# Storing mixer outputs already split in two words, and moving a block's last sums, conditioning loads and weight remainders, in a streaming encoder layer

## The chip, the cores and the metric

The kernel runs on one core of a Trainium2 chip. The metric is the device time of one execution in microseconds. Several executions are timed and the median is given; one further execution is recorded by the hardware profiler.

## The reference

One layer of a hybrid encoder processes a prompt of 2048 tokens and 8 short samples of 16 tokens. A projection feeds two head groups (a gated delta rule and a band attention), their outputs go side by side through `w_out`, and a two-layer FFN follows. The conditioning vector `c` gives shifts, scales and gates through `w_mod`.

```python
sh1, sc1, g1, sh2, sc2, g2 = split(silu(c) @ w_mod + b_mod, 6)
h = rmsnorm(x, norm1_g) * (1 + sc1) + sh1
proj = h @ w_in                                  # 1024 -> 3592 columns
o_a, conv_state, s = mixer_a(proj, ...)          # 4 heads x 128: conv, delta rule, gated norm
o_b = band_attention(proj, ...)                  # 8 heads x 64: own chunk and 8 chunks before
x = x + g1 * (concatenate([o_a, o_b]) @ w_out)
h = rmsnorm(x, norm2_g) * (1 + sc2) + sh2
x = x + g2 * (square(relu(h @ w_up)) @ w_down)   # 1024 -> 4096 -> 1024
```

All is float32, with outputs for the tokens, the states and the newest keys and values.

## The kernel before

Tokens lie in 17 tiles of 128: 16 of the prompt, and tile 16 (`SMP`), which holds all samples. The large products keep float32 precision with words of the type float32r: a number is split into a high word (a cast, on ScalarE) and a low word (the remainder, by a subtraction), and a product is three matmuls, high by high, high by low and low by high (`mm3`). `hT` holds the transposed input of a product, both words, for the tiles of one block.

Weights come by `weights`: the raw slice of 128 x 1024 is loaded into `raw` (3 buffers), ScalarE casts the high word, and GpSimd subtracts for the low word. The first block that meets a slice may store its low word in DRAM (`s_w_in` and others); later blocks then load that word instead of making it. For `w_in`, block 0 makes and stores the low words, and all later blocks load them.

Phase 1 goes through the projections in six blocks, `[0,1,SMP]`, `[2,3,4]`, `[5,6,7]`, `[8,9,10]`, `[11,12,13]` and `[14,15]`. `proj_a` makes the columns of the delta rule (16 slices of `w_in`), `proj_b` those of the attention (12 slices). For the blocks in `LATE` (4 and 2), `proj_b` comes at the end, after that of the last block. The delta rule of earlier blocks (`gdn_*`) is cut into steps that are put between the products (lanes of generators, called by `tick`); so is the attention of the first two tiles. `gdn_o2` transposes a tile's result and stores it in `s_oa`; the attention stores its results in `s_ob`, head by head. 16 pieces of `w_mod` are used at the start; the other 32 (512 KB each) are loaded one by one by `mod_step`, one in each slot of the q, k and v loop of `proj_a` from block 1 on, until none is left.

Phase 2 has five blocks, `[0,1]`, `[2,3,4]`, and three of four tiles. `out_proj` loads each tile's mixer output from `s_oa` and `s_ob` into a buffer `of` (two buffers), splits it into `hT` on ScalarE and VectorE, multiplies by `w_out`, adds to `x1`, and normalizes. `ffn` then alternates four slices of `w_up` with one group of `w_down` (8 groups, each in two halves of 512 columns), summing the groups in `y` on VectorE. At its end come `y * gate + x1` and the store of `y`. The attention of the next block is spread through the FFN. For a block of four tiles, the products of the last `w_down` group come after the last read of `hT` by `w_up`, so the next block's `hT` can be filled beside them.

The program is written in one order, and a planner in the language (it works from a simulated timeline) puts the instructions of each engine, and the DMAs of each queue, in a fixed order when the kernel is built. Nearly all DMAs are issued by the queue of SyncE, in order; a DMA that waits holds back those behind it.

Of the kernel before, what the change touches and what calls it, by code (L numbers as in the profile page):

```python
# [8 lines left out]
F32 = mybir.dt.float32  # L9
# [42 lines left out]
class Trunk:  # L52
    def __init__(self, ctx, tc, ins, outs):
# [10 lines left out]
        self.s_oa = d("s_oa", (NTILE + 1, P, 4, P))  # L64
        self.s_ob = d("s_ob", (NTILE + 1, P, 4, P))
# [100 lines left out]
    def weights(self, name, k0, c0, a, b):  # L166
# [10 lines left out]
        if key in self.stored:  # L177
            nc.sync.dma_start(w.bitcast(F32)[:, 1, 0:n], kept[self.stored[key]][:, 0:n])
            return v(0), v(1)
        self.tt(w[:, 1, 0:n], r, w[:, 0, 0:n].bitcast(F32), ALU.subtract, eng=nc.gpsimd)  # L180
        if self.keep[name]:
            m = sum(k[0] == name for k in self.stored)
            nc.sync.dma_start(kept[m][:, 0:n], w.bitcast(F32)[:, 1, 0:n])
            self.stored[key] = m
# [283 lines left out]
    def proj_a(self, tiles, hT, nxt=()):  # L468
# [38 lines left out]
        for h in range(AH):  # L507
            kq = self.bp.tile([P, 2, self.nt * P], F32, tag="kq", name="kq", bufs=8)
            blk["kq"].append(kq)
            for sec in (1, 0, 2):  # L510
# [28 lines left out]
                if self.bi:  # L539
                    self.mod_step()  # L540
# [329 lines left out]
    def gdn_o2(self, tl, z):  # L870
# [4 lines left out]
        oT = self.tmp("oT")  # L875
        self.act(oT, pt, AF.Copy, scale=self.gdng)
        nc.sync.dma_start(self.s_oa[tl], g4(oT))
# [135 lines left out]
    def conv_gen(self):  # L1013
        nc = self.nc
        for src, w, dst in ((self.hist, 3, self.o["conv_prompt"][0].rearrange("b w c -> (b w) c")),
                            (self.hists, 24, self.o["conv_sample"][0].rearrange("b w c -> (b w) c"))):
            for g in range(3):
# [3 lines left out]
                t = self.tp.tile([P, 512], F32, tag="oT", name="cst", bufs=1)  # L1021
# [4 lines left out]
    def phase1(self):  # L1026
        nc, tc = self.nc, self.tc
        with ExitStack() as st:
# [27 lines left out]
            for bi, tiles in enumerate(B):  # L1056
# [4 lines left out]
                self.drain_to(bi - 2)  # L1061
                blk = self.proj_a(tiles, self.hT, B[bi + 1] if bi in LATE else ())
# [15 lines left out]
            for b, nb in zip(rest, rest[1:] + [None]):  # L1078
                self.proj_b(B[b], self.hT, B[nb] if nb is not None else ())
# [41 lines left out]
    def attention_first(self, tiles):  # L1121
# [53 lines left out]
        def values(h, PT):  # L1175
# [10 lines left out]
            self.tt(o, o, tm[:, 1], ALU.add)  # L1186
            u = h % 2
            for j in range(n):
                nc.sync.dma_start(self.s_ob[tiles[j]][u * 64:(u + 1) * 64, h // 2], o[:, j])
# [20 lines left out]
    def attention_gen(self, tiles):  # L1210
# [67 lines left out]
        def values(h, t, PT):  # L1278
# [5 lines left out]
            tm = ap.tile([64, 256], F32, tag="otmp", name="otmp", bufs=2)  # L1284
            nc.scalar.copy(tm, pv[64:128, 0:256])
            self.tt(tm, tm, pv[0:64, 0:256], ALU.add)
            o = ap.tile([64, P], F32, tag="of", name="of", bufs=2)
            self.tt(o, tm[:, 0:P], tm[:, P:256], ALU.add)
            u = h % 2
            nc.sync.dma_start(self.s_ob[t][u * 64:(u + 1) * 64, h // 2], o)  # L1290
# [33 lines left out]
    def sample_gen(self):  # L1324
# [91 lines left out]
        nc.sync.dma_start(self.s_ob[SMP], oT)  # L1416
# [10 lines left out]
    def out_proj(self, tiles, gates):  # L1427
# [3 lines left out]
        for j, t in enumerate(tiles):  # L1431
            cs = slice(j * P, (j + 1) * P)
            for q, src in enumerate((self.s_oa, self.s_ob)):
                f = self.hp.tile([P, 4, P], F32, tag="htmp", name="of", bufs=2)
                nc.sync.dma_start(f, src[t])
                ks = slice(4 * q, 4 * q + 4)
                self.split(self.hT[:, ks, 0, cs], self.hT[:, ks, 1, cs], f)
# [57 lines left out]
    def ffn(self, tiles, h2, x1):  # L1495
# [3 lines left out]
        y = [self.fp.tile([P, D], F32, tag="y", name="y", bufs=self.nt) for _ in tiles]  # L1499
        G, NF = NGRP, FF // P  # L1500
        us, made = [], 0
        for fi in range(NF + 1):
# [7 lines left out]
            for half in range(2):  # L1510
                hs = slice(half * 512, (half + 1) * 512)
                ws = self.wslices("w_down", g * G, half * 512, 512, G, 2)
                for j in range(n):
# [6 lines left out]
                    else:  # L1520
                        self.tt(y[j][:, hs], y[j][:, hs], ps, ALU.add)
                    self.tick(3 * G * 512)
            us = us[G:]
        self.drain()
        gates = {t == SMP: None for t in tiles}
        for k in gates:
            gates[k] = self.gate_tile(1, k)
        for j, t in enumerate(tiles):
            self.tt(y[j], y[j], gates[t == SMP], ALU.mult)
            self.tt(y[j], y[j], x1[j], ALU.add)  # L1530
            nc.sync.dma_start(self.y_dst(t), y[j])

    def phase2(self):
        nc, tc = self.nc, self.tc
        with ExitStack() as st:
# [4 lines left out]
            self.hT = self.p2.tile([P, KT, 2, self.nt * P], F32R, name="hT2")  # L1540
            for bi, tiles in enumerate(BLOCKS2):
# [5 lines left out]
                x1 = self.out_proj(tiles, [gates[t == SMP] for t in tiles])  # L1547
                if bi + 1 < len(BLOCKS2):
# [6 lines left out]
    def run(self):  # L1555
        self.nraw, self.nw = 3, 4
        self.deferred, self.lanes, self.pending, self.fill_rate, self.fill_acc = [], ([], [], []), [0, 0, 0], 0.0, 0.0
        self.front, self.solved, self.spent = 0, 0, 0
# [38 lines left out]
```

## Time and profile before

| | |
|---|---|
| median of 3 executions | 3190.09 us (3189.9 to 3201.82) |
| the profiled execution, its own time | 3191.66 us |
| its span, first to last instruction | 3190.0 us |
| TensorE busy | 3060.4 us (96%) |
| VectorE, ScalarE, GpSimd busy | 55%, 46%, 19% |
| mean granted TensorE clock | 0.977 |
| DMA | 747 MB, mean 234 GB/s |

Busy times are sums of instruction durations. Matmuls are pipelined, so TensorE counts as busy a little longer than it works; where the granted clock is below 1, the same work takes longer. A window gives the busy time of each engine in a stretch, and the rest of the stretch is idle time.

### The profile page before, as it was taken

The page shows a single profiled execution, that of the slowest core. Times are in us where ns is not written, and L with a number is a line of the kernel's source. Part 1 is how long each engine was busy: PE and PEld are TensorE (multiplying, and loading weights), DVE is VectorE, ACT ScalarE, POOL GpSimd, SP SyncE. Part 2 cuts the span into 40 slices and gives each one's busy share as a digit, 9 for nine tenths or more (in the row PEclk, how much of TensorE's full clock was granted, in tenths as well). Part 3 has the DMA queues.
Part 4 walks back from the last instruction along what each step waited for, and adds up shares of the span by engine and source line. Part 5 has one row for each costly group of instructions (what it writes and reads, how often), then busy time and mean ns, then how long its engine had stood idle before and what let it go on. Part 6 is the DMA issues. An engine that isn't in the chain of part 4 may idle for free. (4 is left out here: it accounts for less than half of the span.)

```text
span 3190.0 us, 53098 instructions
## 1 busy us (share of the span) xinstructions
PE 3060.4 (96%) x19649; PEld 2717.8 (85%) x19649; DVE 1768.1 (55%) x4358; ACT 1471.8 (46%) x2803; POOL 593.5 (19%) x495
## 2 busy tenths in 40 slices
PE   6999999999999989998999999999999999999998
PEld 5998988899989878887999988888988877888887
DVE  4775677777868664675256652444645433442223
ACT  3554545555556555545345453444355333333222
POOL 3631212120212347642222000000000000000000
PEclk8999999999989989998999999999999999999999
DMA  9799897888888768886777766666766667856664
GB/s 295 238 293 300 260 291 221 264 259 245 275 267 272 217 225 268 252 291 192 247 252 246 254 202 188 201 186 205 236 203 200 214 223 228 272 173 196 192 191 139
DMA packets 629116, 747.44 MB, mean 234 GB/s; under 512 B 59680, under 2 KB 483600, under 8 KB 626808
## 3 DMA queue, kind: packets, MB, share of 16 engines
q1 hardware_dynamic: 623096, 712.58, 70.6%
q0 software_dynamic: 5760, 31.46, 3.1%
q8 instruction: 155, 2.54, 0.3%
q14 instruction: 105, 0.86, 0.1%
HBM read 631.29 MB, written 115.52 MB: 234 GB/s over the span
## 5 line engine op out<-in xcount | busy, mean ns | idle before, releaser
L175 ACT CAST w<-raw 128x1024 fp32r<-128x1024 f32 (+1 forms) x528 | 552.0, 1046 | 381.8 <-PE psd L164 212.5
L1479 PE MATMUL psu<-hT,w 128*128 128x512 f32 (+2 forms) x1328 | 471.6, 357 | 4.8 <-ACT hT L104 4.4
L1480 PE MATMUL psu<-hT,w 128*128 128x512 f32 (+2 forms) x1328 | 470.9, 355 | 0.0
L1481 PE MATMUL psu<-hT,w 128*128 128x512 f32 (+2 forms) x1328 | 469.8, 354 | 0.7 <-DMA w<-s_w_up 0.7
L162 PE MATMUL psd<-w,u 128*128 128x512 f32 x1088 | 430.9, 396 | 0.4 <-DVE y L82 0.4
L164 PE MATMUL psd<-w,u 128*128 128x512 f32 x1088 | 429.7, 396 | 0.2 <-DVE u L82 0.2
L163 PE MATMUL psd<-w,u 128*128 128x512 f32 x1088 | 427.2, 393 | 1.8 <-POOL w L82 1.8
L82 POOL TENSOR_TENSOR w<-raw,w 128x1024 fp32r<-128x1024 f32 (+1 forms) x140 | 338.3, 2428 | 269.5 <-ACT w L175 184.5
L79 DVE SCALAR_TENSOR_TENSOR psu<-psu,r 128x512 f32<-128x512 f32 (+2 forms) x160 | 98.8, 617 | 408.1 <-ACT r L92 407.9
L82 DVE TENSOR_TENSOR y<-y,psd 128x512 f32<-128x512 f32 x238 | 162.5, 685 | 251.9 <-PE psd L164 250.6
L1479 PEld LDWEIGHTS psu<-hT,w 128*128 128x128 f32 x1328 | 251.1, 190 | 36.2 <-ACT hT L104 5.3
L1481 PEld LDWEIGHTS psu<-hT,w 128*128 128x128 f32 x1328 | 251.4, 189 | 32.8 <-DMA w<-s_w_up 1.0
L1480 PEld LDWEIGHTS psu<-hT,w 128*128 128x128 f32 x1328 | 251.7, 190 | 30.5 <-issue 0.8
L164 PEld LDWEIGHTS psd<-w,u 128*128 128x128 f32 x1088 | 204.3, 188 | 47.2 <-issue 0.8
L92 ACT ACTIVATE r<-psu 128x512 f32<-128x512 f32 (+2 forms) x160 | 85.4, 533 | 344.1 <-issue 201.8
L163 PEld LDWEIGHTS psd<-w,u 128*128 128x128 f32 x1088 | 204.8, 188 | 46.1 <-POOL w L82 2.2
L162 PEld LDWEIGHTS psd<-w,u 128*128 128x128 f32 x1088 | 204.5, 188 | 44.6 <-DVE y L82 1.0
L162 PE MATMUL psb<-w,hT 128*128 128x256 f32 x816 | 237.1, 291 | 0.3 <-ACT hT L104 0.3
L164 PE MATMUL psb<-w,hT 128*128 128x256 f32 x816 | 234.3, 288 | 2.4 <-DVE hT L82 1.8
L163 PE MATMUL psb<-w,hT 128*128 128x256 f32 x816 | 234.5, 288 | 0.0
L518 PE MATMUL psq<-hT,w 128*128 128x384 f32 (+1 forms) x576 | 195.9, 340 | 9.0 <-ACT ba L498 8.9
L519 PE MATMUL psq<-hT,w 128*128 128x384 f32 (+1 forms) x576 | 194.2, 337 | 0.0
(316 smaller groups left out, 6492.5 us busy)
## 6 DMA issues: line engine op xcount, KB each, us to landing
raw<-in_w_up_dram SPq DMA_DIRECT2D x160, 512.0 KB
raw<-in_w_down_dram SPq DMA_DIRECT2D x160, 512.0 KB
raw<-in_w_in_dram SPq DMA_DIRECT2D x156, 512.0 KB
w<-s_w_in SPq DMA_DIRECT2D x130, 512.0 KB
w<-s_w_down SPq DMA_DIRECT2D x128, 512.0 KB
w<-s_w_up SPq DMA_DIRECT2D x96, 512.0 KB
raw<-in_w_out_dram SPq DMA_DIRECT2D x40, 512.0 KB
x<-in_x_prompt_dram SPq DMA_DIRECT2D x38, 512.0 KB
```

The lines of the kernel that those rows point to most:

```text
L79: (eng or self.nc.vector).scalar_tensor_tensor(out, in0, scalar, in1, op0, op1)
L82: (eng or self.nc.vector).tensor_tensor(out, in0, in1, op)
L92: self.nc.scalar.activation(out, in_, func, **kw)
L162: mm(out, lh, rh, start=first, stop=False)
L163: mm(out, lh, rl, start=False, stop=False)
L164: mm(out, ll, rh, start=False, stop=last)
L175: nc.scalar.copy(w[:, 0, 0:n], r)
L518: mm(pc, wh, hT[:, k, 0, 0:T], start=(k == 0), stop=False)
L519: mm(pc, wh, hT[:, k, 1, 0:T], start=False, stop=False)
L1479: mm(ps[:, c0:c1], wh, h2[:, k, 0, c0:c1], start=(k == 0), stop=False)
L1480: mm(ps[:, c0:c1], wh, h2[:, k, 1, c0:c1], start=False, stop=False)
L1481: mm(ps[:, c0:c1], wl, h2[:, k, 0, c0:c1], start=False, stop=(k == KT - 1))
```

## The change

Four edits are made together.

1. `s_oa` and `s_ob` hold both words. `gdn_o2` casts the high word as before and takes the remainder with one more VectorE instruction from PSUM; it stores two halves. The attention sums its head result in place, splits it there (`split`: a cast on ScalarE, a subtraction on VectorE) and stores two pieces instead of one; `otmp` gets a third buffer and the buffer of the sum goes. `out_proj` loads 512 KB per tile and head group straight into `hT`, with no `of` buffer, cast or subtraction.
2. In `ffn`, `y * gate + x1` is done for each half and tile right behind the last sum. The prompt's gate is loaded once (`gate2`).
3. `mod_step` is called in 32 of the 60 slots of blocks 1 to 5, evenly, instead of the first 32.
4. In the last block of phase 1 (`mix`), every second slice of `w_in` gets its low word from GpSimd again instead of from DRAM: 8 of 16 in `proj_a` and 6 of 12 in `proj_b`.

```diff
@@ weights
         key, kept = (name, k0, c0), self.s_w[name]
-        if key in self.stored:
+        self.turn += self.mix
+        if key in self.stored and not (self.mix and self.turn % 2):
             nc.sync.dma_start(w.bitcast(F32)[:, 1, 0:n], kept[self.stored[key]][:, 0:n])
             return v(0), v(1)
         self.tt(w[:, 1, 0:n], r, w[:, 0, 0:n].bitcast(F32), ALU.subtract, eng=nc.gpsimd)
-        if self.keep[name]:
+        if self.keep[name] and key not in self.stored:
@@ proj_a
-                if self.bi:
+                self.slot += self.bi > 0
+                if self.bi and self.slot * 32 // 60 > (self.slot - 1) * 32 // 60:
                     self.mod_step()
@@ gdn_o2
-        oT = self.tmp("oT")
+        oT, lo = self.tp.tile([P, 512], F32R, tag="oT", name="oT", bufs=1), z.bitcast(F32R)
         self.act(oT, pt, AF.Copy, scale=self.gdng)
-        nc.sync.dma_start(self.s_oa[tl], g4(oT))
+        self.stt(lo, pt, self.gdng, oT.bitcast(F32), ALU.mult, ALU.subtract)
+        nc.sync.dma_start(self.s_oa[tl][:, :, 0], g4(oT.bitcast(F32)))
+        nc.sync.dma_start(self.s_oa[tl][:, :, 1], g4(z))
@@ phase1
                 self.drain_to(bi - 2)
+                self.mix = bi == last
                 blk = self.proj_a(tiles, self.hT, B[bi + 1] if bi in LATE else ())
...
             for b, nb in zip(rest, rest[1:] + [None]):
+                self.mix = b == last
                 self.proj_b(B[b], self.hT, B[nb] if nb is not None else ())
@@ attention_gen, values (attention_first in the same way)
-            tm = ap.tile([64, 256], F32, tag="otmp", name="otmp", bufs=2)
+            tm = ap.tile([64, 256], F32, tag="otmp", name="otmp", bufs=3)
             nc.scalar.copy(tm, pv[64:128, 0:256])
             self.tt(tm, tm, pv[0:64, 0:256], ALU.add)
-            o = ap.tile([64, P], F32, tag="of", name="of", bufs=2)
-            self.tt(o, tm[:, 0:P], tm[:, P:256], ALU.add)
+            o, tr = tm[:, 0:P], tm.bitcast(F32R)
+            self.tt(o, o, tm[:, P:256], ALU.add)
+            self.split(tr[:, P:256], tr[:, 0:P], o)
             u = h % 2
-            nc.sync.dma_start(self.s_ob[t][u * 64:(u + 1) * 64, h // 2], o)
+            for z in range(2):
+                nc.sync.dma_start(self.s_ob[t][u * 64:(u + 1) * 64, h // 2, z], tm[:, (1 - z) * P:(2 - z) * P])
@@ sample_gen
-        nc.sync.dma_start(self.s_ob[SMP], oT)
+        hi = self.sp.tile([P, 4, P], F32R, name="oTh", bufs=1)
+        self.split(hi, oT.bitcast(F32R), oT)
+        nc.sync.dma_start(self.s_ob[SMP][:, :, 0], hi.bitcast(F32))
+        nc.sync.dma_start(self.s_ob[SMP][:, :, 1], oT)
@@ out_proj
-                f = self.hp.tile([P, 4, P], F32, tag="htmp", name="of", bufs=2)
-                nc.sync.dma_start(f, src[t])
-                ks = slice(4 * q, 4 * q + 4)
-                self.split(self.hT[:, ks, 0, cs], self.hT[:, ks, 1, cs], f)
+                nc.sync.dma_start(self.hT.bitcast(F32)[:, 4 * q:4 * q + 4, :, cs], src[t])
@@ ffn
+        gates = {False: self.gate2}
...
                         self.tt(y[j][:, hs], y[j][:, hs], ps, ALU.add)
+                    if g == NF // G - 1:
+                        if SMP in tiles and True not in gates:
+                            gates[True] = self.gate_tile(1, True)
+                        self.tt(y[j][:, hs], y[j][:, hs], gates[tiles[j] == SMP][:, hs], ALU.mult)
+                        self.tt(y[j][:, hs], y[j][:, hs], x1[j][:, hs], ALU.add)
+                        if half:
+                            nc.sync.dma_start(self.y_dst(tiles[j]), y[j])
                     self.tick(3 * G * 512)
             us = us[G:]
         self.drain()
-        gates = {t == SMP: None for t in tiles}
-        for k in gates:
-            gates[k] = self.gate_tile(1, k)
-        for j, t in enumerate(tiles):
-            self.tt(y[j], y[j], gates[t == SMP], ALU.mult)
-            self.tt(y[j], y[j], x1[j], ALU.add)
-            nc.sync.dma_start(self.y_dst(t), y[j])
@@ phase2
+            self.gate2 = self.sp.tile([P, D], F32, name="gate2")
...
                 x1 = self.out_proj(tiles, [gates[t == SMP] for t in tiles])
+                if bi == 0:
+                    nc.sync.dma_start(self.gate2, dram_ap(self.s_gate, (1 + NB) * D, [[0, P], [1, D]]))
```

## Rows read from the trace of the kernel before

**Rows 1.** The page: the span, then busy time and share of each engine.

```profile
span 3190.0 us, 53098 instructions
PE 3060.4 (96%) x19649; PEld 2717.8 (85%) x19649; DVE 1768.1 (55%) x4358; ACT 1471.8 (46%) x2803; POOL 593.5 (19%) x495
```

**Rows 2.** Windows by stage: bounds, length, busy of PE, PEld, DVE, ACT, POOL, clock, DMA, GB/s.

```profile
160.00:640.00 480.00, 467.33 (x3658) 425.67 (x3657) 344.23 (x963) 241.73 (x531) 105.07 (x94) 0.99 0.87 271
640.00:785.00 145.00, 143.47 (x1147) 137.64 (x1147) 107.47 (x322) 80.35 (x181) 26.45 (x24) 1.00 0.82 250
785.00:870.00 85.00, 80.15 (x655) 78.12 (x654) 70.04 (x228) 50.81 (x127) 16.54 (x15) 0.96 0.87 274
870.00:945.00 75.00, 71.28 (x596) 67.24 (x595) 43.10 (x145) 42.81 (x96) 12.58 (x19) 0.82 0.92 293
1110.00:1130.00 20.00, 11.75 (x65) 10.13 (x63) 10.84 (x20) 7.60 (x17) 6.12 (x9) 0.74 0.91 307
1375.00:1410.00 35.00, 30.92 (x187) 27.74 (x187) 31.21 (x42) 15.32 (x25) 16.26 (x8) 0.90 1.00 359
1435.00:1475.00 40.00, 28.20 (x166) 25.43 (x164) 36.08 (x89) 26.91 (x58) 11.78 (x11) 0.82 0.62 199
1765.00:1805.00 40.00, 38.52 (x256) 35.03 (x256) 25.35 (x45) 15.35 (x23) 0.57 (x1) 1.00 0.97 342
2235.00:2275.00 40.00, 40.00 (x246) 35.60 (x245) 26.48 (x41) 14.60 (x22) 0.53 (x1) 1.00 0.88 310
2735.00:2785.00 50.00, 45.17 (x305) 39.28 (x298) 26.85 (x45) 13.52 (x19) 0.00 (x0) 0.93 0.88 287
```

**Rows 3.** Waits of PE over the whole span: total us, times, longest.

```profile
PE pso L162 <- DVE x L82: 7.3, 3, 4.8
```

**Rows 4.** Timeline of VectorE, last 10 us: start us, duration us, line, operation.

```profile
3181.78 0.68 DVE L82 TENSOR_TENSOR y<-y,psd 128x512 f32<-128x512 f32 x1
3184.76 1.22 DVE L82 TENSOR_TENSOR y<-y,x 128x1024 f32<-128x1024 f32 x1
```

**Rows 5.** Timelines of ScalarE, SyncE queue and VectorE around 2770 us.

```profile
2760.00 0.62 ACT L104 CAST hT<-of 128x512 fp32r<-128x512 f32 x1 [6.32 <-DMA of<-s_oa]
2766.72 0.60 SPq L1444 DMA_DIRECT2D x<-in_x_prompt_dram  x1
2779.87 0.42 DVE L82 TENSOR_TENSOR x<-pso,x 128x256 f32<-128x256 f32 x1 [7.71 <-DMA x<-in_x_prompt_dram]
```

**Rows 6.** Tiles of and otmp: instructions, min/median/max ns, first and last start.

```profile
L82 DVE TENSOR_TENSOR of<-otmp x112: 261/282/2781, 1140.4 to 2517.1; 64x128 f32<-64x128 f32 x112
L104 ACT CAST hT<-of x34: 605/621/628, 1110.9 to 2764.8; 128x512 fp32r<-128x512 f32 x34
L82 DVE TENSOR_TENSOR hT<-of,hT x34: 674/692/2867, 1111.6 to 2767.0; 128x512 fp32r<-128x512 f32 x34
L1285 ACT COPY otmp<-pv x112: 362/369/374, 1139.3 to 2516.1; 64x256 f32<-64x256 f32 x112
```

**Rows 7.** Tile oT: instructions.

```profile
L92 ACT ACTIVATE oT<-ptO,gdng x17: 670/687/694, 340.5 to 1103.3; 128x512 f32<-128x512 f32 x17
```

**Rows 8.** Tiles rawx and mrow: instructions.

```profile
L281 SPq DMA_DIRECT2D rawx<-in_w_mod_dram x32: 368/384/1554, 201.0 to 582.0; - x32
L82 DVE TENSOR_TENSOR mrow<-mrow,mps x32: 357/420/423, 227.5 to 604.2; 128x256 f32<-128x256 f32 x32
```

**Rows 9.** DMA issues of one kind: count, size of each.

```profile
w<-s_w_in SPq DMA_DIRECT2D x130, 512.0 KB
```

**Rows 10.** GpSimd groups by line: count, busy us, mean ns, idle before.

```profile
L82 POOL TENSOR_TENSOR w<-raw,w 128x1024 fp32r<-128x1024 f32 x138 | 333.4, 2428 | 260.3 <-ACT w L175 175.3 <-issue 25.7 <-DMA q<-s_q 21.1
```

**Rows 11.** Timelines of GpSimd and VectorE at 141 us, VectorE at 848 us.

```profile
141.32 5.20 POOL L82 TENSOR_TENSOR w<-raw,w 128x1024 fp32r<-128x1024 f32 x2
141.92 2.33 DVE L82 TENSOR_TENSOR E<-E,incl 128x512 f32<-128x512 f32 x1
848.59 0.19 DVE L82 TENSOR_TENSOR ta<-Z,Ds 128x31 f32<-128x31 f32 x1 [4.71 <-DMA Z<-s_A]
```

More of the change, by code (lines that the diff above doesn't have):

```diff
@@ L63, in __init__ @@
         self.s_ext = d("s_ext", (BH, EXT))
-        self.s_oa = d("s_oa", (NTILE + 1, P, 4, P))
-        self.s_ob = d("s_ob", (NTILE + 1, P, 4, P))
+        self.s_oa = d("s_oa", (NTILE + 1, P, 4, 2, P))
+        self.s_ob = d("s_ob", (NTILE + 1, P, 4, 2, P))
         self.s_A = d("s_A", (len(BLOCKS1), 4, AH, 4, 32, 32))
@@ L1020, in conv_gen @@
                     nc.tensor.transpose(ps[0:w, u * P:(u + 1) * P], src[:, g * 4 + u], self.ident)
-                t = self.tp.tile([P, 512], F32, tag="oT", name="cst", bufs=1)
+                t = self.tp.tile([P, 512], F32R, tag="oT", name="cst", bufs=1).bitcast(F32)
                 nc.vector.tensor_copy(t[0:w], ps[0:w])
@@ L1186, in values @@
             self.tt(o, o, tm[:, 1], ALU.add)
+            tr = tm.bitcast(F32R)
+            self.split(tr[:, 1], tr[:, 0], o)
             u = h % 2
             for j in range(n):
-                nc.sync.dma_start(self.s_ob[tiles[j]][u * 64:(u + 1) * 64, h // 2], o[:, j])
+                for z in range(2):
+                    nc.sync.dma_start(self.s_ob[tiles[j]][u * 64:(u + 1) * 64, h // 2, z], tm[:, 1 - z, j])
         load(0)
@@ L1283, in values @@
                 mm(pv[:, 0:256].rearrange("p (z t) -> p z t", z=2), KV[:, w0 + a, 1], PT[:, a], start=(a == 0), stop=(a == m - 1))
-            tm = ap.tile([64, 256], F32, tag="otmp", name="otmp", bufs=2)
+            tm = ap.tile([64, 256], F32, tag="otmp", name="otmp", bufs=3)
             nc.scalar.copy(tm, pv[64:128, 0:256])
             self.tt(tm, tm, pv[0:64, 0:256], ALU.add)
-            o = ap.tile([64, P], F32, tag="of", name="of", bufs=2)
-            self.tt(o, tm[:, 0:P], tm[:, P:256], ALU.add)
+            o, tr = tm[:, 0:P], tm.bitcast(F32R)
+            self.tt(o, o, tm[:, P:256], ALU.add)
+            self.split(tr[:, P:256], tr[:, 0:P], o)
             u = h % 2
-            nc.sync.dma_start(self.s_ob[t][u * 64:(u + 1) * 64, h // 2], o)
+            for z in range(2):
+                nc.sync.dma_start(self.s_ob[t][u * 64:(u + 1) * 64, h // 2, z], tm[:, (1 - z) * P:(2 - z) * P])
         load_k(0)
@@ L1557, in run @@
         self.deferred, self.lanes, self.pending, self.fill_rate, self.fill_acc = [], ([], [], []), [0, 0, 0], 0.0, 0.0
+        self.slot, self.mix, self.turn = 0, False, 0
         self.front, self.solved, self.spent = 0, 0, 0
```

## The prediction

> **What bounds the kernel.** I began with the page: TensorE is busy 96% of the span, the next engine 55% [rows 1]. So the most that any re-ordering can give back is TensorE's idle time, 3190.0 - 3060.4 = 130 us, and what it loses where the clock is granted below 1. Next I read the windows, stage by stage, for three columns: TensorE idle (length less busy), granted clock (a mean of its two levels, 1.2 and 2.4 GHz, so 1.00 is all at 2.4), DMA share [rows 2]. The reader should see three kinds of stretch. In most of phase 1 little is lost: 12.7 us idle in 480 us (160 to 640) and 1.5 in 145 (640 to 785). In the last block of phase 1 more is: from 785 to 870 (its `proj_a`) 4.9 us idle and 0.04 x 85 = 3.4 us of clock; from 870 to 945 (its `proj_b`) 3.7 us idle and 0.18 x 75 = 13.5 us of clock, with the DMA at 0.92 of its time. And at the starts of the phase 2 blocks: 8.3 us idle (1110 to 1130), 4.1 (1375 to 1410), 1.5 (1765 to 1805), none (2235 to 2275), 4.8 (2735 to 2785); DMA 0.88 to 1.00. Last come the waits: the largest of TensorE on `pso` ends with VectorE's `x`, 7.3 us in three waits, one of 4.8 [rows 3]. The timelines say why at 2770 [rows 5]: VectorE's `x` waited 7.7 us for an `x` load issued only at 2766.7, behind the old block's last sums and `y` stores, while ScalarE stood 6.3 us at a cast of `of`.
>
> **The sum, part by part.** Minus is a gain. One engine's added work counts only where TensorE waits for it.
>
> *End of the kernel.* VectorE now ends the last group with four tiles' whole-row products and sums in arrears: the last `psd` sum starts at 3181.78 and the last `y` sum ends at 3184.76 + 1.22 = 3185.98 [rows 4]. With halves done at once, that `psd` sum of 0.68 is followed by two half-size operations, each about 0.68 (a subtraction of 128x512 takes 0.69 [rows 6]): 3183.8. **-2.2 us**, nearly sure.
>
> *Start of the last block (2735 to 2785).* The `x` loads wait for `x1`, freed by the last sums. Those come sooner, and the eight `of` splits, each a cast of 0.62 and a subtraction of 0.69 [rows 6], leave ScalarE and VectorE. To be won: 4.8 us idle and 0.07 x 50 = 3.5 us of clock, 8.3. Against it, eight loads grow from 256 to 512 KB, 2.1 MB more, at the window's 287 GB/s 7.3 us, with 0.12 x 50 = 6 us of DMA time free. Bounds -8.3 to +1.3; the wait was for the order, not for bytes alone, so **-5**.
>
> *Start of block 1 (1375 to 1410).* To be won 4.1 idle and 0.10 x 35 = 3.5. VectorE (31.2 of 35) loses six subtractions of 0.69. But the DMA share is 1.00, and 1.6 MB more at 359 GB/s is 4.4 us. Bounds -7.6 to +4.4; **-1.5**.
>
> *Starts of blocks 2 and 3.* Almost nothing to win (1.5 us). 2.1 MB more is 6.1 us at 342 GB/s and 6.8 at 310; free DMA time 1.2 and 4.8 us. Bounds -1.5 to +6.9 for both; since the first tile needs only a quarter of `hT`, **+2**.
>
> *First block of phase 2 (1110 to 1130).* Before, `of` loads could run ahead of `hT`; now they wait for the space that phase 1's `hT` leaves. 1.0 MB more at 307 GB/s is 3.4 us; two splits less in each tile. Bounds -5 to +5; **+1**.
>
> *Last `proj_b` of phase 1 (870 to 945).* Six low words of 512 KB [rows 9] are no longer loaded: 3.1 MB at 293 GB/s is 10.7 us less of the DMA's 69. At stake are 17.2 us idle and clock. Not all of it is the DMA's, as small products of the delta rule fill that stretch. Bounds -17 to 0; **-7**.
>
> *Last `proj_a` (785 to 870).* Eight low words less (4.2 MB), but about 6.4 loads of `w_mod` more (3.4 MB) and the doubled `s_oa` stores of about three tiles (0.8 MB): the DMA is where it was. VectorE is at 70.0 of 85 us and gets 6.4 row sums of 0.42 [rows 8], three remainders of about 0.69 (like the cast from the same PSUM tile [rows 7]) and the delay behind GpSimd's subtractions, 2.43 us each [rows 10]. How that works is seen at 141 us: a VectorE product of two SBUF operands took 2.33 us beside a GpSimd subtraction [rows 11], against 0.69 for a like size [rows 6], so up to 1.65 us for each of eight, 13 us. Few VectorE instructions have two SBUF operands, so I take 3 in all: **+3**, bounds -8.3 (both losses returned) to +18 (2.7 + 2.1 + 13).
>
> The Trainium skill, "SBUF — State Buffer", section "Who interferes with whom", says that a VectorE instruction with two SBUF inputs contends with a GpSimd instruction that reads SBUF, and that the loser blocks for the whole instruction. The row agrees in kind. As an estimate by that rule, 14 subtractions would cost up to 34 us of VectorE, not the 23 that the row gives; that is no part of the sum.
>
> *Spread `w_mod` loads.* 32 loads ran from 201 to 582 us [rows 8]; now about 19 run in blocks 1 to 3 and 13 later. 6.7 MB at 271 GB/s frees 25 us of DMA time out of 418 (0.87 x 480) before 640. At stake are 12.7 us idle and 4.8 of clock; few of those waits are for weights. Bounds -17.5 to 0; **-2**. In block 4, 3.4 MB more is 13 us, with 0.18 x 145 = 26 free: **+0.5**, up to +3.
>
> *The other 14 remainders in `gdn_o2`.* 14 x 0.69 = 9.7 us of VectorE, which has 480 - 344 = 136 us free from 160 to 640. **+1**, bounds 0 to +9.7. The second store of each is one more issue on SyncE, waited for by nobody until phase 2.
>
> *Attention heads.* Each of 112 units of phase 2 gets one more subtraction (like `of`, 0.28) and one more cast (at most the 0.37 of the copy twice its size) [rows 6]. Both hide under matmuls except where VectorE is full: 1435 to 1475, 36.1 of 40 us, TensorE idle 11.8 [rows 2]. Seven units fall there, 7 x 0.28 = 2. **+2**, bounds 0 to +6 for the like places in later blocks. The 128 added stores of 32 KB are awaited by no engine. The samples' split and the halves of the gate products are below 1 us where they lie.
>
> Sum: -2.2 - 5 - 1.5 + 2 + 1 - 7 + 3 - 2 + 0.5 + 1 + 2 = **-8.2 us**. The profiled execution took 3191.66 us, so 3183.5; that execution is 1.57 above the median, and against 3190.09 the forecast is **3182**.
>
> **The rivals.**
>
> *The DMA was most of the loss.* Evidence: VectorE stood 4.7 us at 848 for a small read-back, `Z` from `s_A`, in a stretch of full DMA [rows 11], and everything behind it stood too. If lighter traffic gives back the whole 17 us of the last `proj_b`, 8 each at the last block's start and in blocks 1 to 3, and 6 at block 1, with +1 for each of first block, last `proj_a` and VectorE, the sum is -2.2 - 17 - 8 - 8 - 6 + 3 = -38: 3152. Against it: the DMA bytes rise elsewhere.
>
> *GpSimd holds VectorE in the last block (slower).* Place: 785 to 945. Price: 14 x 1.65 = 23 us, in place of +3, and the -7 is not won: -8.2 + 20 + 7 = +19, 3209. It decides once VectorE's 70.0 of 85 us grows by more than 15. For it: that share; against: six of the 14 fall after 870, where VectorE has 32 of 75 us free, and few of its instructions have two SBUF operands.
>
> *Block starts wait for bytes.* If all starts pay their upper bound (+1.3, +4.4, +6.9, +5 in place of -3.5), the sum is -8.2 + 3.5 + 17.6 = +13: 3203. For it: shares of 0.97 and 1.00.
>
> *Nothing arrives.* The planner re-orders every queue, gains and losses cancel, the end's 2.2 us stay: 3188.
>
> **Chances.** Forecast 0.34 (own range 3172 to 3192), DMA rival 0.28 (3152 +- 14), GpSimd rival 0.16, bytes rival 0.12, nothing 0.10. 0.5% is 16 us, about what a measurement of this kernel can tell from no change: below 3174 is faster, above 3206 slower. Faster: 0.28 and three tenths of the forecast, 0.38. Slower: two thirds of the GpSimd rival and four tenths of the bytes rival, 0.15. Same: 0.47. For 8 in 10 the range leaves out the lower half of the DMA rival and the upper part of the slow ones: 3151 to 3207.
>
> **What would show it.** In the new profile: the last `y` sum ends about 2 us after the last `psd` sum; the wait of `pso` for `x` is gone and the DMA share at 2735 to 2785 is near 1; the DMA share at 870 to 945 falls below 0.85 and the clock there rises; VectorE's sums of two SBUF operands there lengthen in some places to about 2 us. The prediction is wrong if TensorE's idle time in 870 to 945 stays, if `pso` waits directly for `hT` loads, or if VectorE passes 80 of 85 us in the last `proj_a` with TensorE idle beside it.

## The result, and the profile after

The changed kernel took 3221.89 us at the median (3219.48 to 3228.82, 4 runs) against 3191.34 before (4 runs): a ratio of 1.0088, 95% interval 1.0067 to 1.0108, some 28 us slower. The forecast of 3182 had the wrong sign, and the time lies outside its range of 3151 to 3207.

The page of the kernel after, its span and the busy times, to be read against [rows 1]:

```profile
span 3220.5 us, 53702 instructions
PE 3070.9 (95%) x19649; PEld 2723.8 (85%) x19649; DVE 1816.6 (56%) x4496; ACT 1478.4 (46%) x2890; POOL 628.5 (20%) x509
```

The span grew by 30.5 us. TensorE's busy time grew by 10.5 of them, its idle time from 130 to 150. VectorE has 48 us more work, GpSimd 35. No share of the page says where the loss is, so I read starts of tiles: the first matmul that writes `psg` (gates, at the start and end of each `proj_a`) or `pso` (`out_proj`), to 2 us. From them come the lengths of six stretches that follow each other, in us, for all kernels told of below.

| kernel | blocks 1-3 | block 4, a | last a | from there to first pso | to pso of block 1 | to pso of last block |
|---|---|---|---|---|---|---|
| before | 498 | 70 | 92 | 248 | 276 | 1374 |
| after | 478 | 80 | 112 | 264 | 280 | 1374 |
| e1 spread | 474 | 80 | 106 | 260 | 282 | 1366 |
| e2 mix | 502 | 70 | 104 | 248 | 274 | 1370 |
| e3 split | 502 | 72 | 100 | 258 | 286 | 1374 |
| e4 last sums | 498 | 70 | 90 | 252 | 280 | 1362 |
| e5 null | 494 | 68 | 94 | 246 | 274 | 1374 |
| e6 ahead | 502 | 72 | 100 | 254 | 286 | 1374 |
| e7 split_oa | 502 | 72 | 98 | 258 | 280 | 1368 |
| e8 spread36 | 500 | 70 | 92 | 250 | 278 | 1368 |
| e9 dve_last | 504 | 74 | 90 | 254 | 274 | 1368 |
| e10 dve_mid | 498 | 74 | 92 | 260 | 276 | 1372 |
| e11 heads | 500 | 70 | 90 | 254 | 272 | 1392 |
| e12 split_heads | 500 | 72 | 98 | 254 | 272 | 1414 |
| e13 dve_last2 | 500 | 70 | 92 | 258 | 278 | 1370 |
| e14 dve_mid2 | 494 | 70 | 92 | 246 | 280 | 1374 |
| e15 ob_late | 500 | 70 | 90 | 252 | 276 | 1374 |
| e16 ob_early | 502 | 70 | 90 | 252 | 286 | 1372 |
| e17 mix_b | 506 | 68 | 94 | 252 | 272 | 1368 |
| e18 best | 498 | 68 | 96 | 238 | 282 | 1368 |

One caution goes with it. The planner gives e2 the same order as before up to the first low word of the last block, and yet e2 reached that block at 778 us and before at 770. So a single profile says nothing of differences below some 5 us in a stretch; the verdicts rest on the medians.

After against before: -20, +10, +20, +16, +4, 0. The windows of after for the last block of phase 1, the phases' border and the starts of the later blocks (columns as in [rows 2]):

```profile
682.00:762.00 80.00, 79.62 (x530) 75.33 (x529) 64.14 (x193) 42.68 (x99) 13.17 (x12) 1.00 0.95 279
762.00:874.00 112.00, 102.32 (x893) 92.43 (x891) 89.67 (x252) 55.88 (x138) 39.16 (x26) 0.95 0.72 212
874.00:930.00 56.00, 51.49 (x470) 46.97 (x471) 45.97 (x135) 30.28 (x65) 29.57 (x25) 0.91 0.85 263
874.00:949.00 75.00, 70.49 (x654) 64.70 (x655) 60.07 (x177) 45.74 (x101) 30.33 (x27) 0.93 0.91 285
1124.00:1144.00 20.00, 7.22 (x32) 6.71 (x33) 6.62 (x9) 2.17 (x4) 7.00 (x8) 0.57 1.01 300
1790.00:1830.00 40.00, 38.79 (x259) 35.25 (x258) 25.38 (x54) 12.65 (x22) 0.58 (x1) 1.00 1.07 357
2770.00:2820.00 50.00, 47.31 (x314) 42.01 (x313) 25.85 (x49) 9.93 (x13) 0.00 (x0) 0.93 1.02 327
```

In the last `proj_a` the DMA share is down to 0.72 (0.87 before, 785 to 870), and yet TensorE stands 9.7 us of 112, where it stood 4.9 of 85 [rows 2]; VectorE works 89.7 of 112 us. From 874 to 930 the DMA share is 0.85 at a clock of 0.91. Over 75 us, the length of the window in [rows 2], the clock is up from 0.82 to 0.93, but the DMA share is 0.91 where it was 0.92, and TensorE stands 4.5 us where it stood 3.7: that its idle time there stays was one of the signs that the prediction is wrong. At the border TensorE works 7.2 of 20 us (11.8 before, [rows 2]); at the last block's start the DMA is at 1.02, as forecast. TensorE's waits there, and the SyncE queue just before (start, duration, line):

```profile
PE pso L162 <- DMA hT<-s_oa: 6.9, 1, 6.9
PE ptO L876 <- DVE z L79: 6.1, 1, 6.1
PE pso L162 <- DMA hT<-s_ob: 1.4, 1, 1.4
```

```profile
1132.72 0.52 SPq L881 DMA_DIRECT2D s_oa<-z  x1
1133.34 0.61 SPq L1448 DMA_DIRECT2D hT<-s_oa  x1
1134.00 0.70 SPq L1448 DMA_DIRECT2D hT<-s_ob  x1
```

`pso` waits directly for the `hT` loads, another sign that the prediction named; they are issued right behind the last delta-rule store, as phase 1 ends. That store itself is late: `ptO`, the transposition of the same tile, waited 6.1 us for VectorE's `z`. At the start of the last block a wait of 2.4 us for `hT<-s_ob` stands where 4.8 us for `x` stood [rows 3].

The end went as forecast. VectorE's last 10 us of after:

```profile
3214.32 0.69 DVE L82 TENSOR_TENSOR y<-y,psd 128x512 f32<-128x512 f32 x1 [0.64 <-PE psd L164]
3215.05 0.69 DVE L82 TENSOR_TENSOR y<-y,gate 128x512 f32<-128x512 f32 x1
3215.77 0.69 DVE L82 TENSOR_TENSOR y<-y,x 128x512 f32<-128x512 f32 x1
```

From the start of the last `psd` sum to the end of the last `y` sum it is 2.14 us; it was 4.20 [rows 4].

### The profile page after: what moved, and what is told of

It reads as the page before. It is cut to its first block, busy times and chain, and to the rows that moved or that the text cites. A ratio compares the mean times of both kernels' runs of the same rounds, so it can differ in the third digit from the quotient of the medians.

```text
span 3220.5 us, 53702 instructions
## 1 busy us (share of the span) xinstructions
PE 3070.9 (95%) x19649; PEld 2723.8 (85%) x19649; DVE 1816.6 (56%) x4496; ACT 1478.4 (46%) x2890; POOL 628.5 (20%) x509
## 4 chain that ended last, share of the span: by engine, by line
PE 73%; DMA 11%; DVE 7%; ACT 3%; issue 3%; POOL 2%; SPq 1%; ACTq 0%; POOLq 0%; DVEq 0%
PE psu L1490 7%; PE psu L1492 7%; PE psu L1491 7%; PE psd L164 7%; PE psd L162 7%; PE psd L163 7%; DMA raw<-in_w_up_dram 2%; PE psq L519 2%; PE psb L163 2%; PE psq L520 2%; PE psb L164 2%; PE psq L521 2%; PE psb L162 2%; PE pv L1292 1%; PE psS L1274 1%
## 5 line engine op out<-in xcount | busy, mean ns | idle before, releaser
L82 POOL TENSOR_TENSOR w<-raw,w 128x1024 fp32r<-128x1024 f32 (+1 forms) x154 | 373.7, 2435 | 340.3 <-ACT w L175 289.1
```

The source lines that it names most:

```text
L82: (eng or self.nc.vector).tensor_tensor(out, in0, in1, op)
```

## The experiments

The theories, as the expectations name them. M and G: GpSimd's subtractions hold VectorE, M in the last block of phase 1, G at the attention heads. V: VectorE is on the path of the last `proj_a`. S: the spread moves work into a stretch where it costs more. B: the direct loads cost the phases' border. P: the planner's new order costs by itself, whatever is edited. Times are ratios to before with 95% intervals; 0.1% is 3.2 us.

**One part at a time: e1 to e4.** Each is the kernel before with one of the four edits.

```diff
 e1  -                if self.bi:
     +                self.slot += self.bi > 0
     +                if self.bi and self.slot * 32 // 60 > (self.slot - 1) * 32 // 60:
 e2  +        if key in self.stored and not (self.mix and self.turn % 2):
 e3  +                nc.sync.dma_start(self.hT.bitcast(F32)[:, 4 * q:4 * q + 4, :, cs], src[t])
 e4  +                    if g == NF // G - 1:   # product with the gate and sum, by halves
```

> The kernel before with the wider spread of the w_mod loads alone. Between the two traces, TensorE reached the end of block 3 of phase 1 about 17 us earlier after the change, lost 10 in block 4 and 16 to 20 in the last proj_a. Theory S (the spread moves the load work, it does not take it away): blocks 1 to 3 gain 15 to 18, block 4 loses about 10 and the last proj_a a further 5 to 10, so -2 to +2 us in all. Theory M (GpSimd's subtractions are the price of the last proj_a): the spread alone keeps the -17 and pays the 10 of block 4 only, -7 us. My prediction on record: -1.5 us, with no more than 2 gained in blocks 1 to 3.

Measured: 1.0054 (1.0034 to 1.0074), +17 us. Theory S was right in kind and too small. Blocks 1 to 3 gained 24, then block 4 lost 10, the last `proj_a` 14 and what follows to the first `pso` 12. (The profiled execution took 3203.23 us, the shortest of e1's six, so the table shows less of the loss than the median does.) The end of phase 1 in e1:

```profile
760.00:866.00 106.00, 99.40 (x880) 90.18 (x879) 78.34 (x246) 55.35 (x136) 19.61 (x18) 0.97 0.78 238
930.00:1000.00 70.00, 60.38 (x419) 56.82 (x418) 56.05 (x192) 39.21 (x92) 14.73 (x19) 0.80 0.57 172
```

6.6 us idle in the first; in the second 9.6 idle and a clock of 0.80, with a stretch (930 to 958) in which no `psb` matmul of the projection runs, only small ones. And what left blocks 1 to 3 was TensorE's own work. The stretch from the start of block 1 to that of block 4, before and in e1, first all instructions and then those of the steps' products `mps` alone (PE, PEld, DVE):

```profile
203.00:702.00 499.00, 488.88 (x3847) 447.06 (x3846) 355.29 (x1015) 253.32 (x561) 97.86 (x95) 0.99 0.86 268
203.00:702.00 499.00, 21.36 (x256) 5.17 (x256) 13.28 (x32) 0.99 0.86 268
```

```profile
207.00:682.00 475.00, 464.24 (x3640) 432.32 (x3639) 328.43 (x948) 247.13 (x549) 87.36 (x82) 0.98 0.86 263
207.00:682.00 475.00, 12.14 (x152) 2.99 (x152) 7.92 (x19) 0.98 0.86 263
```

TensorE's idle time in it is 10.1 and 10.8 us, so the whole 24 us is work that went elsewhere: 9.2 are the `mps` products of the moved steps, which my sum had left out, and most of the rest are small products, mainly of the delta rule, that now fall into block 4 (24 of the 72 `pkk` products, some 6 us, are the largest group). They come back there (TensorE busy 68.5 us in block 4 before, 79.4 in e1) and in the last `proj_a` (86.8 and 98.4).

> The kernel before with every second stored low word of the last block made by GpSimd and not loaded, nothing else. Theory M (its subtractions hold VectorE): the last proj_a grows from 58 us to about 70 and the last proj_b gains nothing, +12 to +18 us. Theory S: the last proj_a was slow for the w_mod work that came into it, so here it stays within 4 us of 58 and the sum is -7 to +2 us.

Measured: 1.0005 (0.999 to 1.002), no change. The stretch did grow by 12, as theory M said, but the time did not. The last `proj_a`, before and in e2:

```profile
772.00:864.00 92.00, 87.76 (x751) 84.95 (x750) 72.66 (x230) 53.33 (x130) 18.03 (x15) 0.96 0.82 256
778.00:882.00 104.00, 91.60 (x756) 86.63 (x753) 82.93 (x227) 54.49 (x133) 38.39 (x24) 0.95 0.63 187
```

VectorE takes 82.9 us for 227 instructions where it took 72.7 for 230, and TensorE is idle 12.4 us, with the DMA down to 0.63. The longer ones are sums of two SBUF operands, such as `Ds`, before and in e2:

```profile
L82 DVE TENSOR_TENSOR Ds<-Ds,ta 128x31 f32<-128x31 f32 (+10 forms) x11 | 2.6, 236 | 0.2
L82 DVE TENSOR_TENSOR Ds<-Ds,ta 128x31 f32<-128x31 f32 (+10 forms) x11 | 4.8, 434 | 0.2
```

So GpSimd does hold VectorE here, as theory M has it. The `psb` products of the last `proj_b` and the two late ones then take less time, 231 us (890 to 1121) against 241 (869 to 1110), but the first `pso` comes 8 us behind them, where it came 1 us behind. By itself this part costs nothing that the median shows; the profiled execution is the longest of e2's twelve, 3205.96 us, 10 above that median.

> The kernel before with the attention and delta-rule outputs split where they are made and loaded as two words, nothing else. Theory B (the direct loads into hT can't run ahead of phase 1's end and stand in SyncE's queue behind the last stores): the step from the last proj_b to the first pso grows by about 13 us, the step from block 0 to block 1 by up to 10, +15 to +25 us. Theory M: the step at the phases' border came from VectorE's small products, stretched to 2.3 us beside GpSimd, which exist without the split too; then the split alone costs at most +5 us.

Measured: 1.0092 (1.0069 to 1.0115), +29 us: the size of the whole loss. Theory B's waits are there, `pso` for `hT<-s_oa`:

```profile
PE pso L162 <- DMA hT<-s_oa: 10.6, 2, 7.2
```

They are at most 10.6 of the 29; the table has +8 in the last `proj_a`, +10 up to the first `pso` and +10 in block 0 besides.

> The kernel before with the last sums of a block beside its last products, nothing else. All theories: the end 2.1 us earlier, as in the trace after the change. On the starts of blocks they differ: by the prediction on record the x loads come sooner and the last block's start gains up to 5, so -4 to -7 us; by theory B those starts are bound by the outputs' loads and not by the sums, so -2 us, the end alone.

Measured: 0.9984 (0.9969 to 0.9999), -5 us. The wait of `pso` for `x` at the last block's start fell from 4.8 us in one wait [rows 3] to 2.0 in two. With the 2.1 at the end this fits the forecast for the edit (-4 to -7). But the control e5, which comes next, moves the time as far, so the two places show the gain, and the median does not by itself.

**Controls: e5 and e8.** e5 runs the `w_mod` products one tick later; e8 spreads the steps over the 36 slots of blocks 1 to 3.

```diff
 e5  -            self.later(lambda: self.mod_chunk(*c, rv), 2)
     +            self.later(lambda: self.mod_chunk(*c, rv), 3)
 e8  +                if self.bi and self.slot * 32 // 36 > (self.slot - 1) * 32 // 36:
```

> A control: the kernel before with the 32 w_mod products of blocks 1 to 5 put three ticks behind their slots and not two. No work is added, removed or moved by more than one slot; only the planner gets another order to start from. Theory P (the planner's order alone moves the time by as much as the parts did): 5 to 20 us either way. Theory S and theory B (the parts cost what they move): within 4 us of before.

Measured: 0.9978 (0.9957 to 1.0), -7 us, in the range of theory P, with a bound at no change. A new order alone can be worth some us; a part's effect of that size proves nothing by itself.

> The kernel before with the 32 w_mod steps spread over the 36 slots of blocks 1 to 3 and not over 60: none comes into block 4 or the last block. Theory S (the price of the wide spread is the work brought into block 4 and the last proj_a): within 4 us of before, where the wide spread cost 17. Theory P: 5 to 17 us slower although nothing is moved far.

Measured: 1.0016 (0.9998 to 1.0034), +5, not told from no change. So spreading the steps within blocks 1 to 3 has no such price as e1's; it lies with the work that comes into block 4 and the last block (theory S).

**Where the split costs: e6, e7, e15, e16.** e6 keeps the split and gives block 0 of phase 2 four buffers outside `hT`, with copies; e7 splits the delta rule's output alone; e15 and e16 the heads of tiles 9 to 15 and 2 to 8 alone.

```diff
 e6   +  f = self.hp.tile([P, 4, P], F32R, tag="htmp", name="of", bufs=self.nh)
      +  nc.sync.dma_start(f.bitcast(F32), src[t][:, :, z])   # then a copy into hT
 e7   +  if q == 0:   # s_oa only
      +      nc.sync.dma_start(self.hT.bitcast(F32)[:, ks, :, cs], src[t])
 e15  +  if 9 <= t < SMP:   # e16: 2 <= t < 9
      +      self.split(tr[:, P:256], tr[:, 0:P], o)
```

> The split alone, as in the run e3_split, but block 0 of phase 2 loads both words into four small buffers that exist apart from hT, as before's of did, and copies them into hT (ScalarE the high word, VectorE the low). Theory B: the waits of pso for hT loads at the phases' border, 10.6 us in e3_split, go, and 8 to 13 us of the split's 29 come back. Theory P: the border's waits may go, but the time stays within 5 us of e3_split, as the loss lies in phase 1's order.

Measured: 1.0082 (1.0062 to 1.0102), +26, within the noise of e3. The waits for loads became waits for the copies:

```profile
PE pso L164 <- DVE hT L1452: 5.9, 1, 5.9
PE pso L162 <- ACT hT L1454: 3.9, 2, 3.8
```

Theory B falls as it was put: buffers that let loads run ahead do not give the border's time back. Here the loads of tile 0 did run ahead (issued at 1091 to 1122), but their copies began only at 1134.5, when `hT` was free (its last read, by `psb`, ended at 1132.0), and the loads of tile 1 still came behind the last `s_oa` store, from 1135.8 on.

> The kernel before with the delta rule's output alone split where made (one more VectorE remainder and one more store for each tile); the attention's goes through of as before. The split's loss in e3_split was about 20 us by the end of phase 1 (1112 to 1132) and 8 more at the border. Theory V (VectorE's 17 remainders in phase 1 and the doubled stores are the price): 10 to 20 us in phase 1, here too. Theory B: the border's wait for s_oa stays, so +8 to +13 and no more. Theory P: any number from -5 to +20, with no place of its own.

Measured: 1.0033 (1.0018 to 1.0048), +10 us. The border's wait is there (`pso` for `hT<-s_oa`, 8.8 us), and +10 stands in the stretch up to the first `pso`. The stretch alone would not tell, as e10 below, which leaves the border as it was, has +12 in it. But in e10, as in before, the first `pso` follows the last `psb` product within 1.0 us; in e7 that takes 11.5 us, in e3 7.2 and in after 14.2, with the waits for `hT` told here. (In e2, e8, e13 and e17 it takes 5 to 9 us too, but there TensorE waits for ScalarE's `qs` of the attention.) In e7 `hT` is free when the last `psb` product ends, at 1122.7, and the load is issued behind the last store:

```profile
1128.60 0.61 SPq L879 DMA_DIRECT2D s_oa<-z  x1
1129.30 1.56 SPq L1438 DMA_DIRECT2D hT<-s_oa  x2
```

(The same trace has +6 in the last `proj_a` and -6 from block 1 to the last block, near what single profiles differ by.) The remainder itself took 0.75 us where I had put 0.69:

```profile
L79 DVE SCALAR_TENSOR_TENSOR z<-ptO,gdng,oT x16: 732/746/751, 346.0 to 1118.4; 128x512 fp32r<-128x512 f32 x16
```

> The kernel before with only the attention heads of tiles 9 to 15 split where made and loaded as two words; all other outputs go through of. These heads lie in the FFNs of blocks 2 and 3, where GpSimd is nearly idle (9 and 8 us of 476 and 502). Theory G (the heads' cost is VectorE beside GpSimd): within 5 us of before, where the whole split costs 29 and the delta rule's part of it 10. Theory of the bytes (the rival on record): +6 at the start of the last block, as the trace of e3_split has it. Theory P: anything between -7 and +20.

Measured: 0.9997 (0.9975 to 1.0018). No cost that the interval (-8 to +6 us) tells from none, neither by instructions nor by bytes.

> The same for the heads of tiles 2 to 8 alone, which lie in the FFNs of blocks 0 and 1, beside GpSimd's subtractions of w_up and w_down. Theory G: +8 to +15 us, most of it between block 0's first psu and block 1's pso (214 in before, 222 in e3_split) and in block 1. Theory P: no more than in e15_ob_late.

Measured: 1.0031 (1.0015 to 1.0047), +10 us; +10 in the table from the first `pso` to that of block 1. The same two instructions per head, in e15 (54 or 55 of each) and then in e16, block 0's FFN, by form (count, busy, mean ns):

```profile
L83 DVE TENSOR_TENSOR otmp<-otmp x109: 263/277/285, 1851.4 to 2525.4; 64x128 fp32r<-64x128 f32 x55, 64x128 f32<-64x128 f32 x54
```

```profile
L83 DVE TENSOR_TENSOR otmp<-otmp 64x128 f32<-64x128 f32 x20 | 18.8, 940 | 0.3
L83 DVE TENSOR_TENSOR otmp<-otmp 64x128 fp32r<-64x128 f32 x20 | 18.2, 911 | 0.2 <-ACT otmp L105 0.2
L83 DVE TENSOR_TENSOR otmp<-otmp,pv 64x256 f32<-64x256 f32 x20 | 8.2, 409 | 11.4 <-ACT otmp L1286 11.3
```

Beside the nearly idle GpSimd of e15's stretch none takes more than 0.285 us. Beside its subtractions (152 us busy in that FFN of 220) the remainder takes 0.91 at the mean, 18.2 us in all; the first sum, twice as large but with one operand in PSUM, keeps its 0.41. Theory G holds for this stretch. Its length supports that only in part: 286 us here and in e3 and e6, against 272 to 282 in the kernels that leave these heads alone; but in after it is 280, so how much of the change's own loss lies here is not shown.

**No two SBUF operands: e11, e12.** The head's sums are ordered so that each takes one operand from PSUM; e11 on the kernel before, e12 on the split.

```diff
 e11  -  self.tt(tm, tm, pv[0:64, 0:256], ALU.add)
      +  self.tt(pv[:, 0:P], tm[:, 0:P], pv[:, 0:P], ALU.add)
      +  self.tt(t1, t1, pv[:, P:256], ALU.add)
      +  self.tt(o, pv[:, 0:P], t1, ALU.add)
```

> The kernel before, in which the last sum of an attention head of phase 2 (of <- otmp) takes one operand from PSUM and one from SBUF where it took two from SBUF; this costs one more small sum for each head. In block 0's FFN of before, beside GpSimd's subtractions, that sum took 1.44 us at the median against 0.28 in block 2. Theory G (GpSimd holds VectorE instructions with two SBUF operands): it falls to about 0.3, VectorE loses some 20 us in that FFN, and the FFN with the step to block 1 gains 0 to 5 us. Theory P: the sum's time does not change.

> The split alone, with the head's sum left in PSUM, so that neither the sum nor the remainder of the split has two SBUF operands. Theory G: the remainder and the sum keep 0.28 to 0.4 us beside GpSimd; the 8 us that e3_split lost from block 0's first psu to block 1's pso (222 against 214) come back, and the time is 3205 to 3216. Theory P: within 5 us of e3_split, 3223.

Measured: 1.0101 (1.0077 to 1.0126) and 1.0233 (1.0203 to 1.0264): +32 and +74 us. The mechanism is as theory G has it, the time against it. In e11 none of the 112 sums takes more than 0.285 us, where before's went up to 2.78 [rows 6]:

```profile
L82 DVE TENSOR_TENSOR of<-pv,otmp x112: 261/277/285, 1150.0 to 2568.0; 64x128 f32<-64x128 f32 x112
```

In e12 block 0's FFN took 214 us again (e3: 222), and the stretch from the first `pso` to that of block 1 took 272 (e3: 286). But `out_proj` of blocks 2 and 4 takes 80 and 68 us in e11 (before: 62 and 56), with 25 `pv` matmuls placed into the former in place of 15, and TensorE waits for VectorE's `of` (11.4 us over the span). The result now holds a PSUM buffer one instruction longer; that this is why is argued, not shown.

**VectorE's share: e9, e10, e13, e14.** VectorE work that nothing reads, 128 instructions, in the last `proj_a` (e9, e13) or that of block 2 (e10, e14).

```diff
 e9   +  nc.vector.memset(d, 0.0)   # eight per slice of w_in
 e13  +  nc.vector.tensor_copy(d, w.bitcast(F32)[:, 0, z * P:z * P + P])
```

> The kernel before with eight extra fills of 128x128 by VectorE for each of the 16 slices of the last proj_a, some 0.17 us each by the fills of before (0.91 us for 128x1024, 0.49 for 128x512), about 22 us of VectorE that nothing reads. Theory V (VectorE is on the path of the last proj_a; there the parts added 6.3, 10.9 and 3.5 us to it and 14, 12 and 8 to the stretch): the stretch grows by 15 to 25 us. Theory P (it is the planner's order, in which any part would do the same): -7 to +7 us.

> The same extra fills of VectorE in the proj_a of block 2, where VectorE is at 69 of 88 us and the DMA at 1.00. Theory V as the prediction had it (VectorE is free where the DMA or TensorE is the bound): within 5 us of before. If VectorE is on the path in all of phase 1: 10 to 20 us.

Measured: 1.0056 (1.0036 to 1.0076) and 1.0053 (1.0034 to 1.0071). Neither says what it was made for, as the fills depend on nothing and the planner put all of them first:

```profile
L179 DVE MEMSET dummy<- x128: 165/165/165, 2.6 to 71.5; 128x128 f32 x128
```

> As e9_dve_last was meant: for each of the 16 slices of the last proj_a, eight VectorE copies of 128x128 from the slice's high word, which nothing reads. They can't run before the slice is there (in e9 the planner put all fills into the first 72 us). At some 0.15 to 0.2 us each they are 20 to 25 us of VectorE. Theory V (VectorE is on the path of the last proj_a): that stretch, 92 to 94 us in before and e5_null, grows by 15 to 25, and the time with it. Theory P: the stretch stays below 100 us.

> The same copies in the proj_a of block 2 (378 to 466 us in before, VectorE 69 of 88, DMA 1.00). If only the end of phase 1 hangs on VectorE: that stretch stays within 5 us, and the time too. If VectorE is on the path wherever it passes 0.75 of the time: 15 to 25 us there.

Measured: 1.0033 (1.0018 to 1.0048), +10 us, for the last `proj_a`; 0.9996 (0.9982 to 1.0009) for block 2. The stretches, first e13, then e14:

```profile
774.00:878.00 104.00, 95.65 (x809) 92.28 (x805) 93.03 (x356) 57.20 (x141) 21.28 (x17) 0.95 0.76 231
```

```profile
376.00:462.00 86.00, 83.28 (x532) 74.64 (x534) 78.96 (x281) 40.80 (x94) 12.88 (x11) 1.00 1.02 315
```

In block 2 VectorE is busy 79.0 of 86 us and nothing is lost; at the end of phase 1 the same copies cost 10 (an effect of the order alone, as large as e5's, is not ruled out). That is half of what theory V gave, and not where it put it: the loss stands in the stretch behind the last `proj_a` (+10). A busy share does not tell where an engine is on the path.

**What is left of the change: e17, e18.**

```diff
 e17  +                self.mix = b == last        # before proj_b only
 e18  e17, e4 and e5 together
```

> The kernel before with GpSimd making every second low word of w_in in the last proj_b alone (6 slices), not in the last proj_a. In e2_mix, with both, the last proj_a grew by 12 us (92 to 104) and the last proj_b shrank by 12 (244 to 232), 0 in all. Theory V (VectorE is on the path in the last proj_a only): the 12 of proj_a are not paid, -5 to -12 us. The prediction on record: -7 for this stretch. Theory P: those 12 us moved from one stretch into the other, and this run is within 4 us of before.

> What the runs left of the change: the last sums beside the last products (e4_last, -5 us), the low words by GpSimd in the last proj_b alone (e17), and the w_mod products one tick later (e5_null, -7 us); no split, no wide spread. If the parts add up as theories V and G have it: -12 to -24 us, 3168 to 3180. Theory P (e4's and e5's gains are the luck of one order each): 3180 to 3195.

Measured: e17 0.9993 (0.9975 to 1.0011), e18 0.9939 (0.9916 to 0.9961), 3173.54 us at the median, -19 us: faster than both kernels. Windows of e17 and of e18:

```profile
878.00:930.00 52.00, 46.85 (x461) 44.28 (x461) 40.09 (x113) 32.32 (x70) 25.37 (x21) 1.00 0.86 265
1000.00:1122.00 122.00, 109.48 (x945) 103.11 (x943) 79.43 (x273) 66.78 (x150) 27.75 (x33) 0.96 0.77 238
```

```profile
872.00:930.00 58.00, 53.67 (x540) 50.11 (x539) 44.97 (x120) 37.14 (x79) 25.86 (x22) 1.00 0.89 278
1000.00:1106.00 106.00, 101.04 (x895) 96.51 (x892) 74.31 (x252) 65.45 (x145) 26.51 (x27) 0.98 0.78 242
```

With less DMA the clock around 870 to 930 rose to 1.00 in both (0.82 from 870 to 945 before [rows 2]), as the prediction said. In e17 TensorE is idle 12.5 us from 1000 to 1122 instead (before: 6.5 from 1000 to 1110); in e18 5.0. e17 alone gains nothing, so theory P has that run. e18's interval, -27 to -12 us, holds the sum of its parts measured singly (-5, -7 and -2), as theories V and G had it; but the -7 is the control's, so how much of the gain is the edits' and how much the order's stays open.

## Why the prediction was wrong

The four edits alone sum to 29 + 17 + 1.6 - 5 = 43 us, and together they cost 28; they share the end of phase 1, so the sizes below are those of each edit alone. Three steps of the prediction failed. The largest is the spread of `w_mod`, -1.5 in the sum and +17 measured: what the moved steps cost at their new place was put near nothing. The others are the phases' border with `gdn_o2` (+2, measured +10) and the attention heads (+2, measured +10). Step by step:

*End of the kernel, -2.2, and start of the last block, -5.* The last sums did what was said where the traces show it: 2.1 us at the end, some 3 less of waiting at the last block, -5 at the median of e4. But the second term counted the relief that the direct loads bring as well, and in after `pso` waits for them.

*Attention heads, +2.* The price of the added instruction failed here. I priced the remainder of each unit at 0.28 us, the median of the like sum over the whole span [rows 6], although the same row shows a maximum of 2.78, and although the contention stood in [rows 11] and was used for the last block. In block 0's FFN, 1172 to 1386 us, the trace of before has that sum at a median of 1.44:

```profile
L82 DVE TENSOR_TENSOR of<-otmp x19: 269/1437/2200, 1174.5 to 1382.5; 64x128 f32<-64x128 f32 x19
```

Measured +10 for the heads of tiles 2 to 8, 0 for those of 9 to 15. The rival "GpSimd holds VectorE" had the mechanism, and in e2's trace it is seen at the rival's place too (10 us more of VectorE, +12 in the last `proj_a`); but that edit alone costs no time by the median, and for the heads, where e16 measured a cost, the rival had no price. The Trainium skill, "SBUF — State Buffer", section "Who interferes with whom", names the two conditions, two SBUF inputs and GpSimd reading SBUF; e15, e16 and e11 agree with both, with 0.28 against 0.91 us, and no more than 0.285 where one operand is in PSUM.

*First block of phase 2, +1 (bounds -5 to +5), and `gdn_o2`, +1.* Measured +10 together in e7. I had seen that loads could no longer run ahead, and had priced them by bytes. In e7 and after they wait for their place in SyncE's queue, behind the last delta-rule store; in e3 `hT` itself came free only 1.3 us before the load (1131.6 and 1132.9), so there both hold. At a border with nothing else ready each microsecond counts: from the last `psb` to the first `pso` it is 7 to 14 us, where it was 1. The buffers of e6 did not mend it.

*Spread of `w_mod`, -2 and +0.5.* Mis-sized on both sides: by the trace of e1, -24 in blocks 1 to 3 and +36 from there to the first `pso`; by the median, +17 in all. I took idle time and clock for all that could be won in blocks 1 to 3, and DMA time for all that a step costs in block 4, where 26 us of it were free. The bound of -17.5 was passed although the idle time stayed (10.1 and 10.8 us): what left was TensorE's work, the `mps` products that I had left out and small products of the delta rule, and TensorE, full in block 4, did it there and in the last `proj_a`. Work that is moved is no gain; the loss is what it costs more at its new place, with 9.6 us idle and a clock of 0.80 from 930 to 1000. Why the delta rule's products moved along, no run shows.

*Last `proj_a`, +3, and last `proj_b`, -7.* Together 0 by the median (e2), and the second alone 0 as well (e17). That the two together came near the -4 of the sum is in part luck: in e2's trace VectorE's few sums of two SBUF operands made it 10 us slower in the last `proj_a`, which the prediction took at 3, and of the -7 nothing arrived by the first `pso` (248 us before and in e2). The clock did come back and the time did not, so the rival that the DMA was most of the loss falls too; e18, which gains, holds two other edits.

*Starts of blocks 2 and 3, +2, and of block 1.* From block 1's `pso` to the last block's it is 1374 us before and after, and in e3, which has the doubled loads without the earlier last sums: the doubled loads cost nothing that can be read. In the window at 1790 the DMA is at 1.07 with TensorE idle 1.2 us. The bytes rival falls, as e15 shows too.

Not placed are some 9 of the split's 29 us: e7, e15 and e16 leave them, and block 0's own heads, which lie at the end of phase 1, were not tried alone.

## What to carry to other kernels

Price an instruction that is added by its duration in the stretch where it will stand, not by its median over the span; a median near the minimum with a maximum ten times as long says that place decides. Moving work out of a stretch gains only the difference of two prices, and both must be read; when a stretch gets shorter, look first whether its idle time went or only its work. Where a planner orders the program, run a control with a change that means nothing before believing an effect of a few microseconds, and give filler work an input from the place where it is meant to run.

## What the runs showed of the hardware

A 64x128 VectorE sum of two SBUF operands takes 0.26 to 0.285 us with GpSimd nearly idle (e15), 0.91 to 0.94 at the mean (e16) and up to 4.72 us (after, `otmp`) beside its subtractions of 128x1024; with one operand in PSUM the longest of 112 took 0.285 (e11). The sum of 4.72 us started just behind the first of two such subtractions and ended just behind the second:

```profile
1377.55 4.76 POOL L82 TENSOR_TENSOR w<-raw,w 128x1024 fp32r<-128x1024 f32 x2
1377.74 4.72 DVE L82 TENSOR_TENSOR otmp<-otmp 64x128 f32<-64x128 f32 x1
```

And VectorE busy for 92% of 86 us, beside a DMA share of 1.02, cost the time nothing (e14, 0.9982 to 1.0009).
